# RWKV-7's inverse for two chunks at a time, the chain's output product in its first step, and the moving tiles at one address offset

## The chip, the cores and the metric

The kernel runs on one core of one Trainium2 chip. The metric is the device time of one execution in microseconds (us), as the median of several runs. One execution was also recorded by the hardware profiler; "the span" is its time from the first to the last instruction.

## What is computed

A network of two layers runs over one sequence of 512 rows of width 1024, in float32. Each layer is a half-weighted SwiGLU block, a mixer and another half-weighted SwiGLU block, each behind an RMS norm. The mixer of layer 0 is RWKV-7 on eight heads of 64 beside a block-sparse attention on eight heads; that of layer 1 is HGRN2.

```python
x = x + 0.5 * swiglu(rmsnorm(x, norm_g[l, 0]), ffn1_wg[l], ffn1_wu[l], ffn1_wd[l])
h = rmsnorm(x, norm_g[l, 1])
...
y_a = rwkv7_mix(p[..., :RWKV_COLS], ...)
y_b = moba_mix(p[..., RWKV_COLS:], slopes)
y = jnp.concatenate([y_a, y_b], axis=-1) @ ev_w_out[e]
```

RWKV-7 is a recurrence over time; per head the state is a 64x64 matrix:

```python
sa = jnp.einsum('bhvk,bhk->bhv', state, -kk_t)
state = (state * w_t[:, :, None, :]
         + jnp.einsum('bhv,bhk->bhvk', sa, kk_t * a_t)
         + jnp.einsum('bhv,bhk->bhvk', v_t, k_t))
return state, jnp.einsum('bhvk,bhk->bhv', state, r_t)
```

The kernel cuts the 512 steps into eight chunks of 64. Within a chunk the `sa` of all 64 steps solve a triangular system, so a 64x64 unit triangular matrix per head is inverted, and only the state passes from chunk to chunk.

## The kernel before, in words

**Tiling.** The sequence is cut into two halves of 256 rows, stream A and stream B. Each has its residual tile `x0` or `x1` and its two planes `hh0`, `hl0` or `hh1`, `hl1` of 8 x 256 float32 per partition. A plane pair holds a float32 matrix as a high part and the remainder, both in the reduced type float32r; a product is made of three matrix multiplications, high by high, low by high and high by low (`mm3`, lines 442 to 451). Weights come as units: a raw tile `wr` by DMA, its high part `wh` written by ScalarE, the remainder `wl` by VectorE, with three buffers each. In nearly every unit the weight is the stationary operand and the plane the moving one, with 256 columns: 8 `mm3` over `hh`, `hl` for a gate, up or projection block, 6 `mm3` (8 in the first of the seven parts) over `ah`, `al` for a down block. `ah` and `al` are the planes of the SwiGLU's inner activation, seven buffers each of 256 columns. Only `rows` (lines 691 to 715) has the weight as the moving operand, with 512 columns.

**Where tiles lie.** A pool gives out addresses in the order in which tags first appear. `places` (line 259) fixes the order for the pool `act` in lines 228 to 231: `rqi`, `ms2`, the planes of A, a pad of 32 bytes, the planes of B, `rqz` (four small tiles, 128 bytes together), a pad of 64 bytes, `ah`, `al`, and so on. A plane has 8192 bytes per partition, an `ah` or `al` buffer 1024. The planes of A begin 192 bytes past a multiple of 256; those of B therefore 224 past one, and `ah` and `al`, a further 32 + 128 + 64 - 256 = -32 on from A's offset, 160 past one. The pools of the mixers (`m0` for layer 0, `m1` for layer 1) follow behind this pool.

**Order of the work.** `run` (line 355) walks a list of jobs; a job is one weight unit's products. The small work of norms and mixers is written as generators, "tasks", whose pieces between two `yield`s are steps. After each `mm3`, `fill` (line 313) asks a clock model of the engines which task could go on without waiting, and issues one step of it, so that small products come between large ones in TensorE's one queue. `need` runs a task to its end where a job depends on it. The model only orders the instructions when the program is built.

**RWKV-7.** `rwkv` (line 854) makes the tasks for a pair of chunks: `rw_front` for both, then `rw_prep`, `rw_inv` and `rw_chain` for each. `rw_prep` (line 935) builds the scaled operands, the masked products `Ga` and `Gr`, the transposed operand `BKt`, the identity in `X` and `Xt`, and the inverse's first level. `rw_inv` (line 1000) has five more levels, each in two steps: `zb = Ga^T X` for eight heads, copied to `Z` by ScalarE; then `wt = Z^T Xt` and, but for the last level, `wb = Xt^T Z`, each put into `Xt` or `X` through a mask by VectorE. `rw_chain` (line 1024) has three steps: the product of the state with the chunk's keys into `U`; `Xt` applied to `U`; then the new state, the part `yb` of the output inside the chunk and the part `yc` from the state. Small products of 64 x 64 appear as two records each. The tasks `tail0` to `tail3` finish the output of a pair; the job list has `need tail1` before B's second-last group of projections (line 1352) and `need moba1` before B's output projection (line 1355).

Of the kernel before, what the change touches and what calls it, by code (L numbers as in the profile page):

```python
# [8 lines left out]
F32 = mybir.dt.float32  # L9
F32R = mybir.dt.float32r  # L10
I32 = mybir.dt.int32
U8 = mybir.dt.uint8
AF = mybir.ActivationFunctionType
ALU = mybir.AluOpType
# [7 lines left out]
N = 256  # L22
# [25 lines left out]
RLEV = (1, 2, 4, 8, 16, 32)  # L48
# [142 lines left out]
class K:  # L191
    def __init__(self, tc, ctx, a):
        self.tc, self.a = tc, a
        nc = self.nc = tc.nc
        self.clk = Clock()
        self.pe = Eng(nc.tensor, "pe", self.clk)
        self.v = Eng(nc.vector, "dve", self.clk)
        self.s = Eng(nc.scalar, "act", self.clk)
        self.g = Eng(nc.gpsimd, "pool", self.clk)
        self.q = Eng(nc.sync, "dma", self.clk)  # L200
        self.mm = self.pe.matmul
        self.n = 0
        self.tasks, self.named, self.marks = [], {}, {}
        self.pending, self.micro = [], []
        self.ticks, self.left = 0, 0.0
        self.cp = ctx.enter_context(tc.tile_pool(name="const", bufs=1))
        self.wp = ctx.enter_context(tc.tile_pool(name="wts", bufs=1))
        self.hp = ctx.enter_context(tc.tile_pool(name="act", bufs=1))
        self.ppm = ctx.enter_context(tc.tile_pool(name="pmm", bufs=3, space=PSUM))
        self.ppx = ctx.enter_context(tc.tile_pool(name="pmx", bufs=5, space=PSUM))  # L210
        self.par = self.t(self.cp, [128, NPAR], F32, "par", 1)
        self.cst = self.t(self.cp, [128, NCST], F32, "cst", 1)
        self.msk = self.t(self.cp, [128, NMSK], U8, "msk", 1)
        warm = self.t(self.cp, [128, 1], F32, "warm", 1)
        self.t(self.cp, [128, PAD], U8, "pad", 1)
        self.st = []
        for i in range(2):
            st = Stream()
            st.i = i
            st.x = self.t(self.cp, [128, KT, N], F32, f"x{i}", 1)  # L220
            st.acc = None
            st.hready = 0.0
            self.st.append(st)

        self.places(self.wp, ("wr", KT * 128, F32, 1 + LOADS), ("wh", KT * 128, F32R, AHEAD + 1),
                    ("wl", KT * 128, F32R, AHEAD + 1))
        h = lambda i: [(f"{n}{i}", KT * N, F32R, 1) for n in ("hh", "hl")]
        self.places(self.hp, ("rqi", 8, I32, 4), ("ms2", 2, F32, 2), *h(0), ("pad1", 32, U8, 1), *h(1),
                    ("rqz", 8, F32, 4), ("pad2", 64, U8, 1), ("ah", N, F32R, 7), ("al", N, F32R, 7),
                    ("acc", 2 * N, F32, 1), ("tmp", 2 * N, F32, 2), ("tu", N, F32, 2), ("bc0", N, F32, 1),  # L230
                    ("bc1", N, F32, 1))
        self.q.dma_start(self.st[0].x[:, 0:2], a["x"][0][:, 0:2])
        self.q.dma_start(self.par, a["par"])
        self.g.memset(warm, 0.0)
        self.s.activation(warm, warm, AF.Tanh)
        self.ident, self.id64, self.blk = self.c("ident"), self.c("id64"), self.c("blk")
        self.gmask, self.sel, self.ones = self.c("gmask"), self.c("sel"), self.c("ones")
# [38 lines left out]
        o = PAR[name] + i  # L276
        return self.par[:, o:o + n]

    def rmask(self, i):
        return self.msk[:, i * 64:i * 64 + 64].unsqueeze(1).to_broadcast([128, 4, 64])  # L280

    def hmask(self, i):
        o = NMR * 64 + i * 128
# [570 lines left out]
    def rwkv(self, st):  # L854
        h = st.i
        st.tails = []
        for q in (2 * h, 2 * h + 1):
            env = {}
            st.tails.append((q, env))
            c0, c1 = 2 * q, 2 * q + 1  # L860
            self.spawn(f"fe{q}", self.rw_front(st, q, env), ([f"prep{c0 - 1}"] if q else []) + ([f"tail{q - 2}"] if q > 1 else []))
            for c in (c0, c1):
                self.spawn(f"prep{c}", self.rw_prep(st, c, env),
                           [f"fe{q}"] + ([f"prep{c - 1}"] if c else []) + ([f"chain{c - 2}"] if c > 1 else []))
                self.spawn(f"inv{c}", self.rw_inv(env, c), [f"prep{c}"])
                self.spawn(f"chain{c}", self.rw_chain(env, c), [f"inv{c}"] + ([f"chain{c - 1}"] if c else []))

    def rw_front(self, st, q, env):
        pool, v, s, mm = self.pool, self.v, self.s, self.mm
# [65 lines left out]
    def rw_prep(self, st, c, env):  # L935
        pool, v, s, mm = self.pool, self.v, self.s, self.mm
# [4 lines left out]
        z = env[ci] = {}  # L941

        def p4(tag, w=64, bufs=1):
            return self.t(pool, [128, 4, w], F32, tag, bufs)

        AR = z["AR"] = self.t(pool, [128, 4, 2, 64], F32, "AR", 2)
# [3 lines left out]
        for e in range(2):  # L950
            h = slice(64 * e, 64 * e + 64)
# [11 lines left out]
        Ga = z["Ga"] = self.t(pool, [128, 2, 4, 64], F32, "Ga", 2)  # L963
        Gr = z["Gr"] = self.t(pool, [128, 2, 4, 64], F32, "Gr", 2)
        for e in range(2):
            h = slice(64 * e, 64 * e + 64)
# [3 lines left out]
            for G, i in ((Ga, 0), (Gr, 1)):  # L970
                v.tensor_tensor(G[:, e], gb[:, :, i],
                                self.gmask[:, i * 64:i * 64 + 64].unsqueeze(1).to_broadcast([128, 4, 64]),
                                op=ALU.mult)
# [2 lines left out]
            self.pe.transpose(tb[:, p], BK[:, p], self.ident)  # L976
        BKt = z["BKt"] = p4("BKt", 128, 2)
        s.copy(BKt, tb)
        X, Xt = z["X"], z["Xt"] = p4("X", 64, 2), p4("Xt", 64, 2)
        idb = self.id64.unsqueeze(1).to_broadcast([128, 4, 64])  # L980
        s.copy(X, idb)
        s.copy(Xt, idb)
        yield
        ub = self.bank(4, 64)
        for p in range(4):
# [1 line left out]
            mm(ub[64:128, p], Ga[0:64, 1, p], SV[1][0:64, p], start=True, stop=True)  # L987
        U0 = z["U0"] = p4("U0", 64, 2)
        s.copy(U0, ub)
        ab = self.bank(4, 64)  # L990
        for p in range(4):
            for e in range(2):
                h = slice(64 * e, 64 * e + 64)
                mm(ab[h, p], Ga[h, e, p], self.id64[h], start=True, stop=True)
        v.copy_predicated(X, self.rmask(0), ab)
        for e in range(2):
            h = slice(64 * e, 64 * e + 64)
            v.copy_predicated(Xt[h], self.rmask(len(RLEV))[h], Ga[h, e])

    def rw_inv(self, env, c):  # L1000

        pool, v, s, mm = self.pool, self.v, self.s, self.mm
        z = env[c % 2]
        X, Xt, Ga = z["X"], z["Xt"], z["Ga"]
        he = [(p, e, slice(64 * e, 64 * e + 64)) for p in range(4) for e in range(2)]
        for lv in range(1, len(RLEV)):
            zb = self.bank(4, 64)
            for p, e, h in he:
                mm(zb[h, p], Ga[h, e, p], X[h, p], start=True, stop=True)
            Z = self.t(pool, [128, 4, 64], F32, "Z", 2)  # L1010
            s.copy(Z, zb)
            yield
            wt = self.bank(4, 64)
            for p, e, h in he:
                mm(wt[h, p], Z[h, p], Xt[h, p], start=True, stop=True)
            if lv < len(RLEV) - 1:
                wb = self.bank(4, 64)
                for p, e, h in he:
                    mm(wb[h, p], Xt[h, p], Z[h, p], start=True, stop=True)
                v.copy_predicated(X, self.rmask(lv), wb)  # L1020
            v.copy_predicated(Xt, self.rmask(len(RLEV) + lv), wt)
            yield

    def rw_chain(self, env, c):
        pool, v, s, mm = self.pool, self.v, self.s, self.mm
        z = env[c % 2]
        AR, SV, Xt, Gr, BKt = z["AR"], z["SV"], z["Xt"], z["Gr"], z["BKt"]
        S0 = self.S0
        he = [(p, e, slice(64 * e, 64 * e + 64)) for p in range(4) for e in range(2)]
        sb = self.bank(4, 64)  # L1030
        for p, e, h in he:
            mm(sb[h, p], AR[h, p, 0], S0[h, p], start=True, stop=True)
        U = self.t(pool, [128, 4, 64], F32, "U", 1)
        v.tensor_tensor(U, sb, z["U0"], op=ALU.add)
        yield
        sa = self.bank(4, 64)
        for p, e, h in he:
            mm(sa[h, p], Xt[h, p], U[h, p], start=True, stop=True)
        v.tensor_copy(SV[0][0:64], sa[0:64])
        s.copy(SV[1][64:128], sa[64:128])  # L1040
        yield
        sn = self.bank(4, 64)
        for p, e, h in he:
            mm(sn[h, p], BKt[:, p, h], SV[e][:, p], start=True, stop=True)
        yb, yc = self.bank(4, 64), self.bank(4, 64)
        for p, e, h in he:
            mm(yb[h, p], SV[e][:, p], Gr[:, e, p], start=True, stop=True)
        for p, e, h in he:
            mm(yc[h, p], S0[h, p], AR[h, p, 1], start=True, stop=True)
        S1 = self.t(pool, [128, 4, 64], F32, "S0", 2)  # L1050
        v.tensor_tensor(S1, sn, S0, op=ALU.add)
        v.tensor_tensor(S1, S1, z["EL"].to_broadcast([128, 4, 64]), op=ALU.mult)
        self.S0 = S1
        ys = env["yq"][:, :, (c % 2) * 64:(c % 2) * 64 + 64]
        s.copy(ys, yb)
        v.tensor_tensor(ys, yc, ys, op=ALU.add)

    def rw_tail(self, st, q, env):

# [368 lines left out]
```

## Time and profile before

| | |
|---|---|
| median of 3 runs | 2272.43 us (2269.17 to 2273.28) |
| profiled execution | 2269.33 us, of which the span 2267.4 us |
| TensorE busy, matmuls | 99% of the span, 20476 records |
| VectorE busy | 72% |
| ScalarE busy | 47% |
| GpSimd busy | 0% |
| mean granted TensorE clock | 0.997 of full speed |
| HBM read | 358 MB, 159 GB/s over the span |

A busy share says that something was in flight on an engine, not that it ran at its best pace. Matmul records overlap: each lasts longer than the distance to the next one. So the pace of TensorE is read from the starts, or from how many records fall in a stretch.

### The profile page before, as it was taken

What the parts mean: (1) busy time and instruction counts of PE and PEld (TensorE: products, weight loads), DVE (VectorE), ACT (ScalarE), POOL (GpSimd) and SP (SyncE); (2) the same over time, 40 slices, a digit from 0 to 9 for tenths busy, and PEclk for the clock granted to TensorE, in tenths of its full rate; (3) what the DMA queues carried; (4) which work ended last, traced back from release to release, by engine and by line L of the source; (5) the groups of instructions that cost most, each with busy time, mean ns of one, the idle gap of its engine ahead of it and who ended that gap; (6) DMA issues with size and microseconds to landing.
All of it is one profiled execution on the core that took longest, in us unless ns stands there. A gap on an engine that the chain in (4) does not pass through costs nothing.

```text
span 2267.4 us, 48851 instructions
## 1 busy us (share of the span) xinstructions
PE 2234.2 (99%) x20476; PEld 2164.3 (95%) x20476; DVE 1639.6 (72%) x2863; ACT 1060.6 (47%) x1716; POOL 3.7 (0%) x15
## 2 busy tenths in 40 slices
PE   8999999999999999999999999999999999999998
PEld 8999899899999888999998999999999899999998
DVE  6868758576677666777777776677777777777776
ACT  5545544345554434544454344454455334445444
POOL 0000000000000000000000000000000000000000
PEclk9999999999999999999999999999999999999999
DMA  6565424245544223455654344565655434556564
GB/s 227 184 199 186 167 87 135 90 143 173 187 168 159 83 95 106 140 178 186 185 187 159 122 149 151 185 184 177 190 183 174 143 121 154 168 185 200 186 190 129
DMA packets 107644, 363.64 MB, mean 160 GB/s; under 512 B 12064, under 2 KB 12192, under 8 KB 107296
## 3 DMA queue, kind: packets, MB, share of 16 engines
q1 hardware_dynamic: 107424, 360.53, 49.4%
q8 instruction: 160, 2.62, 0.5%
q14 instruction: 60, 0.49, 0.1%
HBM read 358.38 MB, written 2.10 MB: 159 GB/s over the span
## 4 chain that ended last, share of the span: by engine, by line
PE 92%; DVE 4%; ACT 2%; DMA 1%; issue 1%; SPq 0%; DVEq 0%; ACTq 0%
PE m L176 79%; PE b L176 13%; DVE wl L176 2%; ACT wh L176 1%; DVE acc L176 0%; ACT sh L176 0%; DVE m L176 0%; DVE hl L176 0%; DVE x L176 0%; DVE tmp L176 0%; DMA wr<-in_f1gu 0%; DMA wr<-in_ev_out 0%; DMA wr<-in_f2gu 0%; ACT hh L176 0%; DMA wr<-in_ev_v 0%
## 5 line engine op out<-in xcount | busy, mean ns | idle before, releaser
L176 PE MATMUL m<-hh,wh 128*128 128x256 f32 x3808 | 1090.8, 286 | 12.7 <-ACT wh L176 10.6
L176 PE MATMUL m<-hh,wl 128*128 128x256 f32 x3808 | 1069.5, 281 | 5.4 <-DVE wl L176 5.4
L176 PE MATMUL m<-hl,wh 128*128 128x256 f32 x3808 | 1068.8, 281 | 0.4
L176 DVE TENSOR_TENSOR wl<-wr,wh 128x1024 fp32r<-128x1024 f32 (+2 forms) x725 | 832.0, 1152 | 308.0 <-ACT wh L176 300.2
L176 ACT CAST wh<-wr 128x1024 fp32r<-128x1024 f32 (+2 forms) x725 | 712.3, 990 | 527.6 <-PE m L176 402.2
L176 PEld LDWEIGHTS m<-hh,wh 128*128 128x128 f32 x3808 | 720.5, 189 | 27.5 <-ACT wh L176 11.2
L176 PEld LDWEIGHTS m<-hh,wl 128*128 128x128 f32 x3808 | 721.1, 189 | 7.9 <-DVE wl L176 7.7
L176 PEld LDWEIGHTS m<-hl,wh 128*128 128x128 f32 x3808 | 720.9, 189 | 2.2 <-DVE hl L176 1.2
L176 PE MATMUL m<-ah,wh 128*128 128x256 f32 x1408 | 403.8, 287 | 0.0
L176 PE MATMUL m<-al,wh 128*128 128x256 f32 x1408 | 395.2, 281 | 0.0
L176 PE MATMUL m<-ah,wl 128*128 128x256 f32 x1408 | 395.2, 281 | 0.0
L176 PEld LDWEIGHTS m<-ah,wh 128*128 128x128 f32 x1408 | 265.5, 189 | 7.6 <-issue 5.1
L176 PEld LDWEIGHTS m<-al,wh 128*128 128x128 f32 x1408 | 265.7, 189 | 1.0 <-issue 1.0
L176 PEld LDWEIGHTS m<-ah,wl 128*128 128x128 f32 x1408 | 265.6, 189 | 0.0
L176 ACT CAST ah<-tu 128x256 fp32r<-128x256 f32 x176 | 71.5, 406 | 308.4 <-DVE tu L176 308.3
L176 DVE SCALAR_TENSOR_TENSOR tu<-tu,m 128x256 f32<-128x256 f32 x352 | 146.9, 417 | 6.5 <-ACT tu L176 0.5
L176 DVE TENSOR_TENSOR al<-tu,ah 128x256 fp32r<-128x256 f32 x176 | 74.9, 426 | 84.3 <-ACT ah L176 84.3
L176 DVE SCALAR_TENSOR_TENSOR x<-m,x 128x512 f32<-128x512 f32 x128 | 88.0, 688 | 23.2 <-PE m L176 22.7
L176 DVE TENSOR_TENSOR m<-m,bc 128x512 f32<-128x512 f32 x118 | 81.9, 696 | 17.8 <-PE m L176 15.3
L176 ACT ACTIVATE tu<-m 128x256 f32<-128x256 f32 x176 | 66.7, 379 | 26.7 <-DVE m L176 26.1
L176 PE MATMUL b<-Rq,Rk 128*128 128x128 f32 (+2 forms) x576 | 59.6, 253 | 0.0
L176 PEld LDWEIGHTS b<-Rq,Rk 128*128 128x128 f32 (+2 forms) x576 | 55.3, 168 | 3.8
(204 smaller groups left out, 1456.2 us busy)
## 6 DMA issues: line engine op xcount, KB each, us to landing
wr<-in_f2gu SPq DMA_DIRECT2D x176, 512.0 KB, 3.3
wr<-in_f1gu SPq DMA_DIRECT2D x175, 512.0 KB, 3.8
wr<-in_f1d SPq DMA_DIRECT2D x96, 384.0 KB, 3.2
wr<-in_f2d SPq DMA_DIRECT2D x96, 384.0 KB, 3.2
wr<-in_od_in SPq DMA_DIRECT2D x48, 512.0 KB, 3.2
wr<-in_ev_in SPq DMA_DIRECT2D x44, 512.0 KB, 3.3
wr<-in_f1d SPq DMA_DIRECT2D x16, 512.0 KB, 3.8
wr<-in_ev_out SPq DMA_DIRECT2D x16, 512.0 KB, 3.3
```

The source lines that it names most:

```text
L176: return f(*args, **kw)
```

## The change

The diff has three parts. The tags `pad1`, `pad2` and `rqz` leave the ordered list, so that B's planes follow directly on A's and `ah`, `al` directly on B's; `rqz` gets its address when it is first used, behind `bc1`. All of `hh`, `hl`, `ah` and `al` then begin 192 bytes past a multiple of 256. The mixers' pools begin 96 bytes lower than before, and so does what lies in them. The inverse becomes one task per pair of chunks, on tiles of [128, 8, 64] in place of [128, 4, 64], with its first level taken over from `rw_prep`; it starts when both `rw_prep` are done, and when the chain of the pair before is done. `Z` has one buffer of the double size in place of two. In `rw_chain` the product `yc` and its copy move from the third step to the first, and the addition of `yb` stays in the third.

```diff
-        self.places(self.hp, ("rqi", 8, I32, 4), ("ms2", 2, F32, 2), *h(0), ("pad1", 32, U8, 1), *h(1),
-                    ("rqz", 8, F32, 4), ("pad2", 64, U8, 1), ("ah", N, F32R, 7), ("al", N, F32R, 7),
-                    ("acc", 2 * N, F32, 1), ("tmp", 2 * N, F32, 2), ("tu", N, F32, 2), ("bc0", N, F32, 1),
-                    ("bc1", N, F32, 1))
+        self.places(self.hp, ("rqi", 8, I32, 4), ("ms2", 2, F32, 2), *h(0), *h(1), ("ah", N, F32R, 7),
+                    ("al", N, F32R, 7), ("acc", 2 * N, F32, 1), ("tmp", 2 * N, F32, 2), ("tu", N, F32, 2),
+                    ("bc0", N, F32, 1), ("bc1", N, F32, 1))
...
-                self.spawn(f"inv{c}", self.rw_inv(env, c), [f"prep{c}"])
-                self.spawn(f"chain{c}", self.rw_chain(env, c), [f"inv{c}"] + ([f"chain{c - 1}"] if c else []))
+            self.spawn(f"inv{q}", self.rw_inv(env), [f"prep{c1}"] + ([f"chain{c0 - 1}"] if q else []))
+            for c in (c0, c1):
+                self.spawn(f"chain{c}", self.rw_chain(env, c), [f"inv{q}"] + ([f"chain{c - 1}"] if c else []))
...
-        X, Xt = z["X"], z["Xt"] = p4("X", 64, 2), p4("Xt", 64, 2)
-        idb = self.id64.unsqueeze(1).to_broadcast([128, 4, 64])
-        s.copy(X, idb)
-        s.copy(Xt, idb)
...
-        ab = self.bank(4, 64)
-        for p in range(4):
+
+    def rw_inv(self, env):
+        pool, v, s, mm = self.pool, self.v, self.s, self.mm
+        Ga = [env[i]["Ga"] for i in range(2)]
+        X, Xt = (self.t(pool, [128, 8, 64], F32, n, 1) for n in ("X", "Xt"))
...
+        he = [(i, p, 4 * i + p, e, slice(64 * e, 64 * e + 64)) for i in range(2) for p in range(4) for e in range(2)]
+        ab = self.bank(8, 64)
+        for i, p, j, e, h in he:
+            mm(ab[h, j], Ga[i][h, e, p], self.id64[h], start=True, stop=True)
+        v.copy_predicated(X, self.rmask(0, 8), ab)
...
+        yield
         for lv in range(1, len(RLEV)):
+            zb = self.bank(8, 64)
+            for i, p, j, e, h in he:
+                mm(zb[h, j], Ga[i][h, e, p], X[h, j], start=True, stop=True)
+            Z = self.t(pool, [128, 8, 64], F32, "Z", 1)
             s.copy(Z, zb)
             yield
+            wt = self.bank(8, 64)
+            for i, p, j, e, h in he:
+                mm(wt[h, j], Z[h, j], Xt[h, j], start=True, stop=True)
             if lv < len(RLEV) - 1:
+                wb = self.bank(8, 64)
+                for i, p, j, e, h in he:
+                    mm(wb[h, j], Xt[h, j], Z[h, j], start=True, stop=True)
+                v.copy_predicated(X, self.rmask(lv, 8), wb)
+            v.copy_predicated(Xt, self.rmask(len(RLEV) + lv, 8), wt)
             yield
...
         v.tensor_tensor(U, sb, z["U0"], op=ALU.add)
+        yc = self.bank(4, 64)
+        for p, e, h in he:
+            mm(yc[h, p], S0[h, p], AR[h, p, 1], start=True, stop=True)
+        ys = env["yq"][:, :, (c % 2) * 64:(c % 2) * 64 + 64]
+        s.copy(ys, yc)
         yield
...
-        for p, e, h in he:
-            mm(yc[h, p], S0[h, p], AR[h, p, 1], start=True, stop=True)
...
-        ys = env["yq"][:, :, (c % 2) * 64:(c % 2) * 64 + 64]
-        s.copy(ys, yb)
-        v.tensor_tensor(ys, yc, ys, op=ALU.add)
+        v.tensor_tensor(ys, yb, ys, op=ALU.add)
```

## Rows read from the trace of the kernel before

**Rows 1.** The page: span, and busy time of each engine.

```profile
span 2267.4 us, 48851 instructions
PE 2234.2 (99%) x20476; PEld 2164.3 (95%) x20476; DVE 1639.6 (72%) x2863; ACT 1060.6 (47%) x1716; POOL 3.7 (0%) x15
```

**Rows 2.** The page: the chain that ended last, by engine.

```profile
PE 92%; DVE 4%; ACT 2%; DMA 1%; issue 1%; SPq 0%; DVEq 0%; ACTq 0%
```

**Rows 3.** The page's groups, two of the six large ones: count | busy, mean ns.

```profile
L176 PE MATMUL m<-hl,wh 128*128 128x256 f32 x3808 | 1068.8, 281 | 0.4
...
L176 PE MATMUL m<-al,wh 128*128 128x256 f32 x1408 | 395.2, 281 | 0.0
```

**Rows 4.** Stretches of hh0, hl0 alone: bounds, length, TensorE busy (records), clock, DMA.

```profile
22.00:41.00 19.00, 19.00 (x164) 1.00 0.67 222
105.00:136.00 31.00, 31.00 (x276) 1.00 0.57 189
212.00:239.00 27.00, 27.00 (x240) 1.00 0.57 191
969.00:985.00 16.00, 16.00 (x143) 1.00 0.57 180
1015.00:1036.00 21.00, 21.00 (x181) 1.00 0.55 166
1055.00:1085.00 30.00, 30.00 (x267) 1.00 0.59 186
1104.00:1129.00 25.00, 25.00 (x223) 1.00 0.59 183
1201.00:1221.00 20.00, 20.00 (x179) 1.00 0.67 225
1946.00:1978.00 32.00, 32.00 (x274) 1.00 0.55 178
```

**Rows 5.** The same view, stretches of hh1, hl1 alone.

```profile
577.00:607.00 30.00, 30.00 (x256) 1.00 0.52 179
1543.00:1573.00 30.00, 30.00 (x256) 1.00 0.53 174
```

**Rows 6.** The same view, stretches of ah, al alone.

```profile
1037.00:1053.00 16.00, 16.00 (x137) 1.00 0.67 200
1087.00:1103.00 16.00, 16.00 (x139) 1.00 0.68 201
```

**Rows 7.** Timeline of TensorE around one zb step: start us, us, what.

```profile
275.83 0.28 PE L176 MATMUL m<-hh,wl 128*128 128x256 f32 x1
276.04 0.68 PE L176 MATMUL b<-X,Ga 64*64 64x64 f32 x16
...
276.88 0.28 PE L176 MATMUL m<-hl,wh 128*128 128x256 f32 x1
```

**Rows 8.** The same around one step with wt and wb.

```profile
278.06 0.28 PE L176 MATMUL m<-hh,wl 128*128 128x256 f32 x1
278.26 0.68 PE L176 MATMUL b<-Xt,Z 64*64 64x64 f32 x16
278.78 0.63 PE L176 MATMUL b<-Z,Xt 64*64 64x64 f32 x16
...
279.56 0.28 PE L176 MATMUL m<-hl,wh 128*128 128x256 f32 x1
```

**Rows 9.** Durations (ns min/median/max) and starts: Xt's masked copies; tail1's last write.

```profile
L176 DVE COPY_PREDICATED Xt<-msk,b x40: 431/436/447, 281.3 to 871.5; 128x256 f32<-128x256 uint8 x40
...
L176 DVE TENSOR_TENSOR hl<-yq,hh x1: 693/693/693, 479.7 to 479.7; 128x512 fp32r<-128x512 f32 x1
```

**Rows 10.** Timeline of TensorE where B's first unit of rows begins.

```profile
563.09 0.40 PE L176 MATMUL m<-wh,hh 128*128 128x512 f32 x1
```

**Rows 11.** The page's group of the largest small products, out of moved tiles.

```profile
L176 PE MATMUL b<-Rq,Rk 128*128 128x128 f32 (+2 forms) x576 | 59.6, 253 | 0.0
L176 PEld LDWEIGHTS b<-Rq,Rk 128*128 128x128 f32 (+2 forms) x576 | 55.3, 168 | 3.8
```

More of the change, by code (lines that the diff above doesn't have):

```diff
@@ L277, in p, with rmask @@
         return self.par[:, o:o + n]
-    def rmask(self, i):
-        return self.msk[:, i * 64:i * 64 + 64].unsqueeze(1).to_broadcast([128, 4, 64])
+    def rmask(self, i, n=4):
+        return self.msk[:, i * 64:i * 64 + 64].unsqueeze(1).to_broadcast([128, n, 64])
     def hmask(self, i):
@@ L989, in rw_prep @@
         s.copy(U0, ub)
-        ab = self.bank(4, 64)
-        for p in range(4):
+    def rw_inv(self, env):
+        pool, v, s, mm = self.pool, self.v, self.s, self.mm
+        Ga = [env[i]["Ga"] for i in range(2)]
+        X, Xt = (self.t(pool, [128, 8, 64], F32, n, 1) for n in ("X", "Xt"))
+        for i in range(2):
+            env[i]["Xt"] = Xt[:, 4 * i:4 * i + 4]
+        idb = self.id64.unsqueeze(1).to_broadcast([128, 8, 64])
+        s.copy(X, idb)
+        s.copy(Xt, idb)
+        he = [(i, p, 4 * i + p, e, slice(64 * e, 64 * e + 64)) for i in range(2) for p in range(4) for e in range(2)]
[3 more added lines that the diff above has]
+        v.copy_predicated(X, self.rmask(0, 8), ab)
+        for i in range(2):
@@ L992, in rw_prep @@
             for e in range(2):
                 h = slice(64 * e, 64 * e + 64)
[L994 to L1005, printed above, removed]
+                v.copy_predicated(Xt[h, 4 * i:4 * i + 4], self.rmask(len(RLEV))[h], Ga[i][h, e])
@@ L1006, in rw_inv @@
+        yield
         for lv in range(1, len(RLEV)):
-            zb = self.bank(4, 64)
-            for p, e, h in he:
-                mm(zb[h, p], Ga[h, e, p], X[h, p], start=True, stop=True)
-            Z = self.t(pool, [128, 4, 64], F32, "Z", 2)
+            zb = self.bank(8, 64)
+            for i, p, j, e, h in he:
+                mm(zb[h, j], Ga[i][h, e, p], X[h, j], start=True, stop=True)
+            Z = self.t(pool, [128, 8, 64], F32, "Z", 1)
             s.copy(Z, zb)
             yield
-            wt = self.bank(4, 64)
@@ L1014, in rw_inv @@
-            for p, e, h in he:
-                mm(wt[h, p], Z[h, p], Xt[h, p], start=True, stop=True)
+            wt = self.bank(8, 64)
+            for i, p, j, e, h in he:
+                mm(wt[h, j], Z[h, j], Xt[h, j], start=True, stop=True)
             if lv < len(RLEV) - 1:
[L1017 to L1021, printed above, removed]
+                wb = self.bank(8, 64)
+                for i, p, j, e, h in he:
+                    mm(wb[h, j], Xt[h, j], Z[h, j], start=True, stop=True)
+                v.copy_predicated(X, self.rmask(lv, 8), wb)
@@ L1044, in rw_chain @@
             mm(sn[h, p], BKt[:, p, h], SV[e][:, p], start=True, stop=True)
-        yb, yc = self.bank(4, 64), self.bank(4, 64)
+        yb = self.bank(4, 64)
         for p, e, h in he:
             mm(yb[h, p], SV[e][:, p], Gr[:, e, p], start=True, stop=True)
-        for p, e, h in he:
-            mm(yc[h, p], S0[h, p], AR[h, p, 1], start=True, stop=True)
         S1 = self.t(pool, [128, 4, 64], F32, "S0", 2)
```

## Prediction, made before the changed kernel was run

> **What bounds the kernel now.** I read the page first. TensorE has matmuls in flight for 99% of the span [rows 1], and 92% of the chain that ended last lies on it [rows 2]. So time is won where TensorE issues faster or issues less, and a shorter step on VectorE or ScalarE is worth nothing by itself. The bulk of TensorE's work is six groups of float32r products with 256 moving columns: three groups of 3808 on `hh` or `hl`, half of them for each stream, and three of 1408 on `ah` or `al`; one of either kind stands in [rows 3]. That makes 5712 products on A's planes, 5712 on B's and 4224 on `ah`, `al`.
>
> Their pace is in none of these rows, because records overlap. I counted records in stretches where one kind runs alone. A record of 0.28 us [rows 3] that crosses an edge is counted too, so the distance between two starts is (length + 0.28) / records. On A's planes [rows 4], which begin 192 bytes past a multiple of 256, two paces appear: 31.28 / 276 = 113.3 ns and 30.28 / 267 = 113.4 ns in six of the nine stretches, 19.28 / 164, 21.28 / 181 and 32.28 / 274 = 117.6 to 117.8 ns in three. On B's planes, at 224, both stretches have 30.28 / 256 = 118.3 ns [rows 5]. On `ah`, `al`, at 160, there are 16.28 / 137 = 118.8 and 16.28 / 139 = 117.1 ns [rows 6], on average 118.0. The granted clock is 1.00 of full speed (2.4 GHz) in all of them, so the clock is not the difference. It isn't the DMA either: the six move 180 to 225 GB/s, the three 166 to 222. The rows on `ah` show that the half of the network isn't it: 1037 to 1053 lies in the same stage of A as 1055 to 1085, with the same weights' buffers. What is left is the moving tile, and with it its address. At 192 TensorE has two paces, 113.4 and 117.7 ns, and keeps one over a whole stretch; at the other two offsets the short one doesn't appear.
>
> **The placement.** I take it that all three kinds behave after the change as A's planes do now. Records of [rows 4]: 1328 in the stretches at 113 ns and 619 in those at 118, so 68%, about two thirds, go at the short distance, and the mean is 0.68 x 113.4 + 0.32 x 117.7 = 114.8 ns. Then B's planes win 118.3 - 114.8 = 3.5 ns x 5712 = 20.0 us, `ah` and `al` win 3.2 ns x 4224 = 13.5 us, and A's planes win nothing. Sum 33.5 us. All of it lies on the path, since nothing covers TensorE; and the weights keep up, because A's stretches already run at 113.4 ns without a gap. What I can't read is the share of the short pace afterwards: it is set by what happens where a stretch begins. With one half at 113.4 the sum is 4 us lost on A, 16 and 10 us won, 22 us; with 85% it is 45 us. These are the bounds of the forecast.
>
> The Trainium skill would have none of this: the page "SBUF — State Buffer", section "Specifications (TRN2)", speaks of lines of 16 bytes, of which 160, 192 and 224 are all multiples, and the page "TensorE: Matmul & The Clock Gate", section "Back-to-back issue gap", has the distance as columns / 2.4 GHz + 2.5 ns, 109.2 ns for 256 columns, with no term for an address. By both the placement would be worth nothing. The rows disagree by 5 ns at one clock, and I go by the rows.
>
> The mixers' tiles move down by 96 bytes. Nothing shows what that does. Nearest are HGRN2's products, 59.6 us of records with their weight loads in flight for 55.3 us of it [rows 11]. Were they to change by the 4% between the two paces of [rows 4], it would be 2.4 us either way. I take nothing, because the loads, whose pace doesn't hang on the moving tile, fill nearly the whole time.
>
> **The inverse for two chunks.** Each step that `fill` puts between large products costs TensorE more than its own products. Around a `zb` step two large products on either side start 276.88 - 275.83 = 1.05 us apart [rows 7]; two distances of 0.12 us would be there anyway, so the step costs 0.81 us for its 16 records. With `wt` and `wb`, 32 records, it is 279.56 - 278.06 = 1.50, less 0.24, 1.26 us [rows 8]. So 16 records cost 0.45 us and each step a further 0.36 us, whatever its size. Before, a pair of chunks has 2 x 10 steps of the inverse and 2 third steps of `rw_prep` that hold the first level; afterwards 10 steps, one more for the first level, and the 2 steps of `rw_prep`: 22 become 13, while the number of products stays. That saves 9 x 0.36 = 3.2 us a pair, 12.8 us over four pairs. Bounds: nothing, where steps of two chunks already stand back to back and share that price (the rows show them apart); 4 us a pair, 16 us in all, if the two steps of `rw_prep` that lose the first level found room beside others.
>
> VectorE does one masked copy of 512 columns where two of 256 stood. These take 0.44 us each; a 512-column operation from the same engine takes 0.69 us [rows 9], so it wins 0.2 us a copy. ScalarE's copies change alike. Both lie beside TensorE's stream, and count nothing. They do lengthen one step's way from product to product by about 0.25 us on either engine, and that meets the wait that the change adds: the inverse now waits for both `rw_prep` and the chain of the pair before, and behind it wait the chains, the `tail` and at last `need tail1`. `tail1` writes its last plane at 479.7 us [rows 9], and B's units with 512 columns, which stand ahead of that `need` in the list, begin only at 563.1 us [rows 10]. So 83 us of large products cover a late chain; nothing counts.
>
> **The chain.** `yc` moves from the third step to the first, 16 records each way, 0.45 us off and 0.45 us on; ScalarE's copy and VectorE's addition keep their number. No step is added or lost: zero, within 0.1 us a chunk, below 1 us in all. No DMA is added or moved, and SP's queue keeps its order.
>
> **The sum.** 33.5 + 12.8 = 46.3 us. The profiled execution took 2269.3 us, so it would take 2223; the median of the runs is 3.1 us above that execution, and so the forecast is 2272.4 - 46.3 = 2226 us. With the bounds of that share it lies between 2272 - 22 - 13 = 2237 and 2272 - 45 - 13 = 2214 us.
>
> **The rivals.**
> - *All at 113.4 ns.* Where `hh` and `ah` follow each other at the same offset nothing might push TensorE out of the short pace any more. For: A's pace changes across the stretch of `ah` between 1036 and 1055 us [rows 4]. Against: the same rows have three stretches at 117.7 and that offset, from 22 to 1978 us. The sum: 1.4 x 5712 + 4.9 x 5712 + 4.6 x 4224 = 55 us, with the inverse 68, thus 2204 us. Chance 0.14.
> - *`ah`, `al` don't follow.* They are seven small buffers, rewritten all the time. Then 20.0 + 12.8 = 33 us, 2240 us. Chance 0.08.
> - *The address is not the cause*, but what else sets these tiles apart (their place in the memory, or their writers). Then the first part doesn't do what its words say, and 12.8 us are left: 2260 us. This is what the two pages of the skill amount to. Against it stands that A's planes differ from B's in nothing else that the rows show. Chance 0.13.
> - *All at 117.7 ns.* The whole stream falls into the long distance of [rows 4]: A's planes lose 2.9 x 5712 = 16.6 us, the others win 0.6 x 5712 + 0.3 x 4224 = 4.7, and with the inverse it is 2272 - 1 = 2271 us, no change. Chance 0.04.
> - *The chain comes late*, the one that ends slower. The place is `need tail1`. It decides once a half's RWKV-7 ends more than 83 us later than now. The rest then runs with no large product beside it, each step waiting for a copy on the way to `Z` and back, some 0.7 + 0.7 us [rows 9]. A half has 2 x 11 + 4 x 3 = 34 such steps; bare in both halves they cost 68 x 1.4 = 95 us, against 46 won: 2321 us. Against it stands the cover, as a step grows by 0.5 us only, 34 x 0.5 = 17 us. Chance 0.02.
>
> **How the numbers follow.** The forecast has the remaining 0.59. The range should leave out no more than 0.2: from the first rival to the one where `ah` doesn't follow, 0.14 + 0.59 + 0.08 = 0.81, with a few us at the ends for the terms taken as nothing, 2202 to 2246 us. A measurement of this kernel tells 0.2%, some 4.5 us, from no change. Faster by more are all cases but the last two, 0.94; no change 0.04; slower 0.02.
>
> **What would show it.** In the stretches of B's planes and of `ah`, 113 to 114 ns in about two thirds and 117.7 in the rest, and none at 118.3 with A's planes as they are now. In the timeline steps of 32 `X`, `Ga` records at 1.26 us and of 64 at 2.2 us, 11 a pair. `tail1` done well ahead of B's rows of 512 columns, and the idle time of TensorE unchanged. I am wrong if B's planes still show 118.3 ns, or if TensorE waits for `wh` or `wl` in those stretches.

## The result, and the profile after the change

The changed kernel takes 2244.08 us (median of four runs, 2235.81 to 2252.18) beside 2270.8 us for the kernel before in the same comparison: a ratio of 0.9882, with an interval from 0.984 to 0.9923, or 27 us less. The forecast of 46 us less was too much. The range held the result by 2 us, and by luck: the bounds that were worked out from the share of the short pace, 2214 to 2237 us, missed it, and the range reached to 2246 us only because a rival that did not come true (`ah` doesn't follow) was taken in. Its runs lie 16 us apart, those of the kernel before 5. The profiled execution took 2247.7 us. The page of the kernel after, which answers to [rows 1] and [rows 2]:

```profile
span 2245.7 us, 48723 instructions
...
PE 2211.2 (98%) x20476; PEld 2148.2 (96%) x20476; DVE 1633.4 (73%) x2823; ACT 1056.6 (47%) x1688; POOL 3.7 (0%) x15
...
PE 90%; DVE 5%; ACT 2%; issue 1%; DMA 1%; SPq 0%; DVEq 0%; ACTq 0%
```

TensorE still sets the end, with the same 20476 matmul records; VectorE has 40 instructions fewer and ScalarE 28. The stretches that answer to [rows 4 to 6] come in the order A's planes, B's planes, `ah`, B's planes, B's planes, `ah` (bounds, length, TensorE busy with its records, granted clock, DMA share, GB/s):

```profile
108.00:138.00 30.00, 30.00 (x257) 1.00 0.61 188
571.00:601.00 30.00, 30.00 (x268) 1.00 0.58 192
...
1025.00:1040.00 15.00, 15.00 (x130) 1.00 0.67 201
1531.00:1561.00 30.00, 30.00 (x257) 1.00 0.53 169
2094.00:2122.00 28.00, 28.00 (x249) 1.00 0.62 189
2126.00:2140.00 14.00, 14.00 (x126) 1.00 0.73 201
```

By (length + 0.28) / records B's planes now go at 30.28 / 268 = 113.0 ns or at 30.28 / 257 = 117.8, `ah` at 14.28 / 126 = 113.3 or 15.28 / 130 = 117.5, and nothing is left at 118.3 or above. From the starts of all records the two distances are 113.33 and 117.78 ns for every kind, a stretch keeps its own through changes from `hh` to `ah` and back, and it changes only where small products or a wait come between, if only one that makes a single distance 125 to 160 ns long. That is what the prediction said of the offset. What it had wrong stands in the first row: A's planes between 108 and 138 us are at the long distance, where the kernel before had them at the short one. Of the products in undisturbed stretches 44% go at 113.3 ns, not 68%.

The steps of the inverse, from the same timeline views as [rows 7] and [rows 8]; first `zb` for two chunks:

```profile
297.56 0.28 PE L176 MATMUL m<-hh,wl 128*128 128x256 f32 x1
297.76 1.15 PE L176 MATMUL b<-X,Ga 64*64 64x64 f32 x32
...
299.06 0.29 PE L176 MATMUL m<-hl,wh 128*128 128x256 f32 x1
...
304.39 0.28 PE L176 MATMUL m<-hh,wl 128*128 128x256 f32 x1
304.60 1.15 PE L176 MATMUL b<-Xt,Z 64*64 64x64 f32 x32
305.58 1.10 PE L176 MATMUL b<-Z,Xt 64*64 64x64 f32 x32
...
306.84 0.28 PE L176 MATMUL m<-hl,wh 128*128 128x256 f32 x1
```

32 records cost 299.06 - 297.56 - 0.24 = 1.26 us and 64 cost 306.84 - 304.39 - 0.24 = 2.21 us, as worked out before from steps of half the size.

### The profile page after: what moved, and what is told of

It reads as the page before. It is cut to its first block, busy times and chain, and to the rows that moved or that the text cites. A ratio compares the mean times of both kernels' runs of the same rounds, so it can differ in the third digit from the quotient of the medians.

```text
span 2245.7 us, 48723 instructions
## 1 busy us (share of the span) xinstructions
PE 2211.2 (98%) x20476; PEld 2148.2 (96%) x20476; DVE 1633.4 (73%) x2823; ACT 1056.6 (47%) x1688; POOL 3.7 (0%) x15
## 4 chain that ended last, share of the span: by engine, by line
PE 90%; DVE 5%; ACT 2%; issue 1%; DMA 1%; SPq 0%; DVEq 0%; ACTq 0%
PE m L176 78%; PE b L176 12%; DVE wl L176 2%; ACT wh L176 1%; DVE x L176 0%; DVE tmp L176 0%; DMA wr<-in_f1gu 0%; DVE m L176 0%; ACT sh L176 0%; ACT hh L176 0%; DVE hl L176 0%; DMA wr<-in_ev_v 0%; DVE rqz L176 0%; DVE acc L176 0%; ACT tmp L176 0%
## 5 line engine op out<-in xcount | busy, mean ns | idle before, releaser
L176 PEld LDWEIGHTS m<-hh,wh 128*128 128x128 f32 x3808 | 723.3, 190 | 23.9 <-ACT wh L176 12.3
L176 PEld LDWEIGHTS m<-ah,wh 128*128 128x128 f32 x1408 | 265.9, 189 | 10.7 <-issue 7.4
```

The costliest lines, as they stand in the source:

```text
L176: return f(*args, **kw)
```

## The experiments

Wherever a distance is given for a whole run, it is worked out from the starts of its large products with 256 columns, some 15 000 of them next to one another.

### The placement alone

The kernel before, with the new list of tags:

```diff
-        ... *h(0), ("pad1", 32, U8, 1), *h(1), ("rqz", 8, F32, 4), ("pad2", 64, U8, 1), ("ah", N, F32R, 7), ...
+        ... *h(0), *h(1), ("ah", N, F32R, 7), ...
```

> The kernel before, with the changed list of tags alone (no pads, rqz later); the inverse stays one task a chunk. Theory: the moving tiles' offset allows two paces, 113.3 and 117.8 ns, and the changed kernel's 22 to 28 us are the sum of a part from the paces and about 10 us from 36 steps fewer. Then this kernel takes 10 us more than the changed one, about 2254 us, 13 to 18 below the kernel before, and its runs differ from one another by several us, as those of the changed kernel do. Rival (the pair of chunks is what won): within 5 us of the kernel before, 2266 to 2271 us.

Measured: 2253.03 us (2252.41 to 2257.72) against 2272.2; ratio 0.9918, from 0.9904 to 0.9931, 19 us less. Stretches of B's planes:

```profile
580.00:610.00 30.00, 30.00 (x267) 1.00 0.58 191
1398.00:1428.00 30.00, 30.00 (x257) 1.00 0.56 178
```

One is at 30.28 / 267 = 113.4, the other at 117.8 ns, at the same clock of 1.00. The placement wins by itself, about what the theory gave it. (Its 19 us and the 15 us of the next run add up to more than the 27 us of both together, but the interval of the changed kernel has room for that: 0.9918 x 0.9935 = 0.9853.) Its runs differ by 5 us, less than the changed kernel's, so the spread is not shown by this run.

### The pair of chunks alone

The changed kernel with the old list of tags, so with the old offsets:

```diff
-        ... *h(0), *h(1), ("ah", N, F32R, 7), ...
+        ... *h(0), ("pad1", 32, U8, 1), *h(1), ("rqz", 8, F32, 4), ("pad2", 64, U8, 1), ("ah", N, F32R, 7), ...
```

> The changed kernel with the old list of tags: B's planes at 224, ah and al at 160. Theory: 36 steps fewer at 0.3 us, 10 us won: 2258 to 2262 us; in its stretches B's planes at 118.3 ns and A's at 113.3 or 117.8. Rival (the pair of chunks is what won): 2244 us as the changed kernel.

Measured: 2257.61 us (2255.19 to 2260.66); ratio 0.9935, from 0.9921 to 0.9948, 15 us less. A stretch of A's planes, then one of B's:

```profile
1043.00:1073.00 30.00, 30.00 (x268) 1.00 0.58 185
1395.00:1425.00 30.00, 30.00 (x256) 1.00 0.57 177
```

B's planes are back at 30.28 / 256 = 118.3 ns. The mean distance of the run is 117.06 ns, that of the kernel before 117.02, so the 15 us aren't won in the large products. Between 240 and 1000 us the traces have 191 visits to small products before (a visit is a group of small products between two large ones) and 157 here. Over the whole trace the visits of the inverse take 10.7 us less, those of the chain 1.2. So 12 of the 15 us are the inverse and the chain; the other 3 are within what single executions of either kernel differ by.

### All tiles at 224, or on a multiple of 256

The changed kernel with a pad of 32 bytes ahead of A's planes, or one of 64:

```diff
-        ("ms2", 2, F32, 2), *h(0), *h(1), ...
+        ("ms2", 2, F32, 2), ("padx", 32, U8, 1), *h(0), *h(1), ...
```

> The changed kernel with 32 bytes ahead of A's planes, so that all of hh, hl, ah, al begin 224 past a multiple of 256. Theory: the offset is the cause; no stretch at 113.3 ns, all at 118.3, A's planes too: 15648 products at 118.3 in place of 115.9 ns cost 38 us on the changed kernel's 2244, so about 2280 us. Rival (not the offset, but the place in the memory or the neighbours): paces and time as in the changed kernel, 2236 to 2252 us.

> The changed kernel with 64 bytes ahead of A's planes: all of hh, hl, ah, al on a multiple of 256. If what matters is a multiple of 64 bytes, the two paces 113.3 and 117.8 ns and 2236 to 2252 us as in the changed kernel. If it is the distance from the weights' tiles, which also begin on a multiple of 256, other paces, slower ones: 118 ns throughout, about 2280 us.

Measured: 2276.21 us with 32 bytes and 2297.01 us with 64, one run each. A's planes at 224, and then, from the other trace, at 0:

```profile
1054.00:1084.00 30.00, 30.00 (x256) 1.00 0.57 180
```

```profile
1063.00:1093.00 30.00, 30.00 (x253) 1.00 0.56 175
```

30.28 / 256 = 118.3 ns at 224, where A's planes had 113.4 before, and 30.28 / 253 = 119.7 ns at 0 (120.0 from the starts, in every stretch). The tiles moved by 32 and 64 bytes and kept their order, neighbours and writers. So the offset is the cause, and not the place in the memory. The second run is 53 us above the changed kernel with nothing but 64 bytes between them.

### The weights moved as well

```diff
-        self.places(self.wp, ("wr", KT * 128, F32, 1 + LOADS), ("wh", ...
+        self.places(self.wp, ("wr", KT * 128, F32, 1 + LOADS), ("padw", 64, U8, 1), ("wh", ...
```

> The changed kernel with 64 bytes ahead of wh and wl: the weights begin 64 past a multiple of 256, and hh, hl, ah, al on one, as in the kernel that gave 119.9 ns, so that the distance from weights to moving tiles is 192 modulo 256, as in the changed kernel. Theory 1 (the distance to the weights decides): two paces, 113.3 and 117.8 ns, 2236 to 2252 us. Theory 2 (the moving tile's own offset decides): 119.9 ns throughout and about 2297 us.

Measured: 2244.06 us, one run. B's planes, then A's:

```profile
513.00:538.00 25.00, 25.00 (x223) 1.00 0.59 179
1040.00:1070.00 30.00, 30.00 (x257) 1.00 0.59 186
```

25.28 / 223 = 113.4 and 117.8 ns, though the moving tiles begin on a multiple of 256 as in the run that had 120.0. What decides is the distance from the stationary operand's tile to the moving one's. "192 bytes past a multiple of 256" is right in this kernel because its weights begin on one. That the distance counts modulo 256 is not shown: the products of a unit step through the weights by 512 bytes and through the planes by 1024, all at one pace, so it counts modulo 512 at most, and no two tiles compared here differ by 256. Offsets below are given modulo 256 only to name them.

### The other multiples of 64

For 64 the pad has 128 bytes; for 128 `ms2` moves behind `bc1`.

> The changed kernel with 128 bytes ahead of A's planes: hh, hl, ah, al 64 past a multiple of 256, the weights on one. Both theories leave the pace open; offsets so far: 160 gave 117.3 and 118.7, 192 gave 113.3 and 117.8, 224 gave 118.3, 0 gave 119.9 ns. If pace only falls away from 192 on both sides, 118 ns or more and 2270 us or more.

> The changed kernel with ms2 moved behind bc1: hh, hl, ah, al 128 past a multiple of 256. As for 64: open; if pace only falls away from 192, 117.5 ns or more and 2265 us or more; if 128 holds one pace of 113.3 ns, 2244 - 15000 x 2.6 ns = 2205 us.

Measured: 2263.51 us at 64 and 2280.63 us at 128, one run each. Two stretches of A's and B's planes at 64, then two of A's at 128:

```profile
1050.00:1080.00 30.00, 30.00 (x268) 1.00 0.63 190
1400.00:1430.00 30.00, 30.00 (x257) 1.00 0.57 178
```

```profile
107.00:137.00 30.00, 30.00 (x253) 1.00 0.59 184
1056.00:1086.00 30.00, 30.00 (x255) 1.00 0.56 180
```

At 64 the same two distances appear as at 192; the run is longer because only 14% of the products go at 113.3 ns. At 128 there are 119.7 and 118.7. My expectation that the pace only falls away from 192 is wrong: 64 and 192 are the two good ones among the six offsets seen, and no offset gave 113.3 ns alone.

### What ends a visit

The share of 113.3 ns is what the forecast missed, so I asked the traces what stands ahead of a stretch (of 15 products or more). In the changed kernel every one of the 11 stretches behind a sum of squares (`inv_rms`, products of all 128 output rows by one column) goes at 117.8 ns, and all 8 behind HGRN2's products of 32 output rows at 113.3. The first try makes the norm's small products in halves of 64 output rows:

```diff
-            self.mm(bc[:, j], st.r[:, j:j + 1].to_broadcast([128, 128]), self.ident, start=True, stop=True)
+            for e in range(2):
+                self.mm(bc[64 * e:64 * e + 64, j], st.r[:, j:j + 1].to_broadcast([128, 64]), self.ident,
+                        start=True, stop=True)
...
-                self.mm(ss[:, j:j + 1], st.acc[k // 2][:, k % 2, j * 128:(j + 1) * 128], self.ones,
-                        start=k == 0, stop=k == m - 1)
+                for e in range(2):
+                    o = j * 128 + 64 * e
+                    self.mm(ss[64 * e:64 * e + 64, j:j + 1], st.acc[k // 2][:, k % 2, o:o + 64], self.ones,
+                            start=k == 0, stop=k == m - 1)
```

> The changed kernel, with the norms' small products made in halves of 64 output rows (inv_rms and spread), so that the visit to the norm ends in a product that fills half of the array's columns. In the changed kernel's trace a visit that ends in the sum of squares is followed by 117.8 ns every time, and one that ends in a half-sized product mostly by 113.3. Theory (what ends a visit sets the pace of the stretch behind it): the share of 113.3 rises from 44% to 70% or more, 15000 x 0.26 x 4.4 ns = 17 us or more, 2215 to 2227 us. Rival (the pace is drawn anew each time, whatever ended): 2236 to 2252 us.

Measured: 2247.93 us (2242.26 to 2255.06), ratio 0.989 from 0.9869 to 0.9911: no gain on the changed kernel. Behind the sums in halves 8 of 9 stretches go at 113.3 ns, where none did. Behind `spread` in halves, which follows some us later and ends in products of 128 columns, it is 7 of 12, no better than the 9 of 13 behind whole ones in the changed kernel. `spread` stands ahead of the long stretches, so the share stayed at 43%. (The 11 of 13 in the next expectation is an earlier count of the same trace.) The theory's number failed and its mechanism was half shown: the ending counts, but not by its rows alone.

The second try keeps the sums in halves, leaves `spread` whole, and ends 23 visits (every `spread`, the last of `hg_out`, of `moba` for a half and of `rw_tail`) with two products of 64 rows by one column that nobody reads:

```diff
+    def settle(self):
+        d = self.bank(1)
+        for e in range(2):
+            self.mm(d[64 * e:64 * e + 64], self.ident[:, 64 * e:64 * e + 64], self.ones, start=True, stop=True)
```

> The changed kernel with the sums of squares in halves as in the run before, and two further products of 64 output rows and one column, written to a bank that nobody reads, behind spread, behind the last product of hg_out, of moba for a half and of rw_tail: some 24 places. In the run before, 11 of 13 stretches behind a sum of squares in halves went at 113.3 ns; behind spread in halves only about half, and behind hg_out (848 and 733 products) none. Theory (what ends a visit sets the pace): most of the five stretches of 700 to 1560 products go at 113.3, the mean falls from 115.9 to 114.5 or less, 21 us, less 24 x 0.15 us: 2222 to 2230 us. Rival (the pace is drawn at each visit, with the ending of no account): 2236 to 2252 us plus the 4 us of the added products.

Measured: 2230.45 us (2228.21 to 2236.02) against 2272.45; ratio 0.9818, from 0.9803 to 0.9833. Its interval lies below that of the changed kernel; it is the shortest of all that ran. One of the places, the last products of `hg_out` and what follows, first in the changed kernel, then here:

```profile
1389.04 1.05 PE L176 MATMUL b<-cst,rqy 128*128 128x128 f32 x8
1389.84 0.37 PE L176 MATMUL m<-ah,wh 128*128 128x256 f32 x1
1390.05 0.28 PE L176 MATMUL m<-al,wh 128*128 128x256 f32 x1
```

```profile
1382.83 1.05 PE L176 MATMUL b<-cst,rqy 128*128 128x128 f32 x8
1383.81 0.28 PE L176 MATMUL b<-cst 128*64 128x1 f32 x4
1384.02 0.39 PE L176 MATMUL m<-ah,wh 128*128 128x256 f32 x1
1384.24 0.28 PE L176 MATMUL m<-al,wh 128*128 128x256 f32 x1
```

The stretch behind it, in the same run:

```profile
1387.00:1417.00 30.00, 30.00 (x267) 1.00 0.60 183
```

The way from the small products' start to the second large one grows from 1390.05 - 1389.04 = 1.01 to 1384.24 - 1382.83 = 1.41 us, so each place costs 0.40 us, more than the 0.15 expected. It pays from some 90 products on, at 4.45 ns each, where the stretch would else have gone at 117.8. The 848 products behind this place went at 117.8 ns in the changed kernel and go at 30.28 / 267 = 113.4 here. Behind the added products 19 of 23 stretches go at 113.3, and 79% of all undisturbed products in the run; its mean distance is 114.29 ns, against 115.89 in the changed kernel. That is 1.6 ns x 15 000 = 24 us, less 23 places at 0.40 us, 9 us: 15 us net; measured are 2244.1 - 2230.5 = 14 us. The added products do not always leave the short distance: two stretches of 117 products, one in each half, went at 113.3 ns without them and go at 12.28 / 104 = 118 here:

```profile
1329.00:1341.00 12.00, 12.00 (x104) 1.00 0.51 171
1858.00:1870.00 12.00, 12.00 (x104) 1.00 0.52 171
```

## Why the prediction was right or wrong

**What bounds the kernel.** Right: every run that won or lost did so in TensorE's distances or in its visits.

**The placement.** The step that the offset allows the short pace, and that B's planes and `ah` would behave as A's, held to a tenth of a ns; the runs at 224, 0 and with the weights moved show it. The step that failed is the share: "so 68%, about two thirds", taken for all three kinds. As a reading of A's planes before the change it was right: over that whole trace 67% of their undisturbed products go at the short distance. It did not carry over, not even to A's planes themselves: in the changed kernel's trace they have 40%, B's 49%. So A's planes, which were to win nothing, went from 114.9 to 116.0 ns and lost 6 us; B's went from 118.3 to 115.6 and won 15 in place of 20.0; `ah`, `al` went from 118.0 to 116.1 and won 8 in place of 13.5. That makes 17 us in place of 33.5, below my lower bound of 22 us, which stood for one half, as 44% is below one half. Four long stretches decide it: 1315 products from 987 us, 848 from 1390, 1558 from 1498 and 733 from 1928 are all at 117.8 ns.

The share is no matter of chance either. In layer 1 both halves do the same work in turn, and in the changed kernel's trace they have the same 26 stretches behind small products, from 1243 us on and from 1782 us on. All 26 go at the same distance in both halves, 18 of them at the short one. Of the 26 in A's half, the run with the placement alone and the one with `inv_rms` and `spread` in halves have all 26 at the same distance as here, the one with the weights moved 23. Two of them, each in A's half and in B's:

```profile
1336.00:1348.00 12.00, 12.00 (x108) 1.00 0.45 158
1874.00:1886.00 12.00, 12.00 (x108) 1.00 0.53 170
1400.00:1430.00 30.00, 30.00 (x257) 1.00 0.58 176
1938.00:1968.00 30.00, 30.00 (x257) 1.00 0.57 171
```

108 records in 12 us are 113.7 ns, 257 in 30 us are 117.8. So the distance goes with what stands ahead of a stretch, and mostly repeats. What in it decides is open, and so is why the changed kernel's runs lie 16 us apart, as one execution of each kernel was traced.

What A's planes lost can be seen in [rows 4] and [rows 6]. Between 1015 and 1085 us they go from 117.6 to 113.4 ns with nothing but `ah` between, at its other offset. The prediction counted that for "All at 113.4 ns", as if `ah` pushed TensorE out of the short pace; here it had led out of the long one. In the trace before, A's planes follow directly on 60 or more products of `ah` seven times, and six of the seven are at the short distance; in the run with the pair alone, which has the old offsets, it is again six of seven, and A's planes keep 61%. With all tiles at one offset a stretch takes its distance through `ah` in all 16 places of the changed kernel's trace. The same stage, A's planes before and behind the `ah` of 1025 to 1040 us:

```profile
993.00:1023.00 30.00, 30.00 (x257) 1.00 0.56 176
1043.00:1073.00 30.00, 30.00 (x257) 1.00 0.58 180
```

That this is why A's share fell is a reading of the traces; no run tried it by itself.

**That the address is not the cause.** The runs at 0 and at 192 lie 53 us apart, and over six offsets the distances reach from 113.3 to 120.0 ns at a clock of 1.00; that rival falls. By the Trainium skill the placement would be worth nothing: "SBUF — State Buffer", section "Specifications (TRN2)", has lines of 16 bytes, of which all six offsets are multiples, and "TensorE: Matmul & The Clock Gate", section "Back-to-back issue gap", has no term for an address. The runs disagree, by the 113.3 to 120.0 ns above, and the measurement decides. The 109.2 ns of the prediction should not have been put against this stream: the page gives that formula for single products, and for a stream of weight loads and products it has some 81 ns at 128 columns and 131 at 512, and no figure for 256.

**The inverse.** Right in kind, a little large: 36 visits fewer in the whole trace (306 and 270), as counted, and 1.26 and 2.21 us as worked out. Over the whole trace the five levels fall from 79.7 to 65.9 us, but the first level costs 2.7 us more as a step of its own: 11.0 us won in place of 12.8. The term that was mis-sized is that first level, put at 0.45 us per chunk where it stood in `rw_prep`. The step that held it, 32 records, before the change:

```profile
272.97 0.28 PE L176 MATMUL m<-hh,wl 128*128 128x256 f32 x1
...
274.31 0.28 PE L176 MATMUL m<-hl,wh 128*128 128x256 f32 x1
```

It cost 274.31 - 272.97 - 0.24 = 1.10 us and costs 0.81 without the level, so taking it out gave back only 0.29. The price of a visit is nearer 0.34 than 0.36 us: 0.81, 1.27 and 2.20 us for 16, 32 and 64 records.

**The chain.** `yc` cost a little less than nothing: the first step of a chain rose from 0.81 to 1.27 us, the third fell from 1.89 to 1.28, 0.15 us less per chunk and 1.2 us in all, by the trace. It wasn't tried by itself. The mixers' tiles, 96 bytes lower and taken as nothing, were nothing: no kind of HGRN2's visits changed by more than 0.15 us in sum.

**The late chain.** The rival put the longer steps at 17 us in a half, and the chain comes 18 us later; that the longer steps are what delays it, and not the added wait, is not shown. The last write of `tail1`, before at 479.7 us [rows 9]:

```profile
L176 DVE TENSOR_TENSOR hl<-yq,hh x1: 692/692/692, 497.8 to 497.8; 128x512 fp32r<-128x512 f32 x1
```

Nothing waits for it, as B's units of 512 columns now begin at 558 us.

**What else.** By the starts of all records the paces save 1.13 ns x 14 990 undisturbed distances (under 0.16 us) = 16.9 us, the inverse 11.0, the chain 1.2 and the other visits 2.5. That is 31.6 us, but the two profiled spans differ by 21.7. The rest, 9.9 us, went back to longer distances between two large products with no visit between: 95 of them are over 0.16 us before the change and 158 after. About 2.9 of it lies at the start. A load on the chain landed later, by the chain of waits (start, duration) of the kernel before and then of the kernel after:

```profile
4.01 6.29 DMA wr<-in_f1gu
```

```profile
4.01 7.95 DMA wr<-in_f1gu
...
14.34 4.84 PE m L176 x21
```

TensorE began as early as before, at 6.4 in place of 6.1 us, but its first products last 0.41 us and lie 0.21 us apart, nearly twice the later distance: 256 columns at the lower of its two levels, 1.2 GHz, though the clock column reads 1.00 there. With the waits between them that goes on to 18.6 us, where the kernel before was at the short durations from 12.7 us on; first the kernel after, then the kernel before:

```profile
18.56 0.41 PE L176 MATMUL m<-hh,wh 128*128 128x256 f32 x1
```

```profile
12.66 0.28 PE L176 MATMUL m<-hh,wh 128*128 128x256 f32 x1
```

That makes 46 such products in place of 23, and TensorE's long run began 2.8 us later (24.5 in place of 21.7 us). The nine experiments' traces have the change between 9.5 and 14.8 us, so this is of the one execution and not of the kernel. Another part is TensorE's own waits for the weights' planes (total, times, longest), where the kernel before had 11.0 and 6.1 us:

```profile
PE m L176 <- ACT wh L176: 11.9, 7, 6.4
PE m L176 <- DVE wl L176: 7.7, 13, 0.9
```

That is 2.5 us more; that the faster TensorE meets the splitting of weights more often is the likely reason, and not shown. What else is in the 9.9 us is not traced. My prediction that TensorE's idle time stays as it was is wrong by these 2.5 us.

**The rivals.** Neither "all at 113.4 ns" nor "all at 117.7 ns" came true, and `settle` shows that one can go toward the first on purpose. "`ah`, `al` don't follow" is refuted by the rows of 113.3 and 117.5 ns on `ah`.

## What to carry to other kernels

Where TensorE's stream sets the time, read its distance from start to start, stretch by stretch and tile by tile, before anything else; busy shares and mean durations hid 4% here. Try the moving tile's offset against the stationary one's, and when a stretch shows two paces, don't take their mix for a property of the layout: look at what stands ahead of each stretch, and whether it can be ended otherwise. A share read from one layout need not carry over to another: here it was 67% for A's planes before and 40% after. Merging two small steps into one is worth the fixed price of a visit to small products, 0.34 us here, times the visits saved, and no more.

## What the runs showed of the hardware that was not expected

- The distance between float32r products of 256 columns, by the offset of the moving tile from the stationary one (named modulo 256 bytes), at a granted clock of 1.00: 120.0 ns at 0; 113.3 or 117.8 at 64; 118.7 or 120.0 at 128; 117.3 or 118.7 at 160; 113.3 or 117.8 at 192; 118.3 at 224.
- Which of the two holds is fixed at the start of a stretch and stays for up to 1558 products, 180 us. Sums with 128 output rows by one column left the long distance 11 times of 11 in the changed kernel; the same sums in halves left the short one 8 of 9 and 7 of 10 times in the two runs that had them. In layer 1 the 26 distances of one half are those of the other.
- Why the distance between the two tiles counts was not measured and stays open; that moving both by 64 bytes gives back the two distances of the changed kernel shows that it is the one against the other, and no more.
- Two added products of one column cost 0.40 us, though they hold only four records.
- At the start of the changed kernel's profiled execution 46 large products ran at nearly twice the later distance, up to 18.6 us, and 23 in the kernel before, up to 12.3 us; the clock column shows 1.00 in both.
